# A two-layer decoder trunk: new order of the first loads, shared normalised input for the gate, and regrouped state-output products

## The chip, the cores and the metric

One NeuronCore of a Trainium2 chip runs the whole kernel in one launch. The metric is device time in microseconds (us), lower is better. TensorE, VectorE, ScalarE and GpSimd appear in the profile as PE (matmuls), PEld (weight loads of PE), DVE, ACT and POOL; SP is the engine that issues most DMAs, and its own queue is SPq.

## What is computed

The input x is 256 x 1024 in float32. Layer one is a diagonal complex state-space mixer, layer two an attention mixer over one block of 256 keys. Cut to the first layer, which is what the change touches:

```
hn = rms_norm(x, g)
u, z = split(hn @ w_in)                # 256 x 1024 each
a = exp(dt * (a_re + i a_im))          # 64 groups x 64 states, dt = exp(log_dt)
s = scan(a, f * (u B))                 # state over 256 steps
y = gelu(Re(s C) + d * u)              # back to 1024 channels
y = y * sigmoid(y @ w_glu + b)         # "GLU"
h = x + (y * silu(z)) @ w_out
```

## The kernel before

The program is first recorded, then ordered, then emitted. Every call on an engine handle becomes an `Op` in `Program.add` with a cost in ns from a formula (lines 155 to 176) and its dependences. `Program.order` computes for each Op a priority `way` (six rounds of forward and backward list scheduling in `lay`); `lay` takes on each engine the ready Op with the largest `way`. The emitted order on each engine is fixed from then on, so a change of a cost formula can move instructions anywhere in the kernel, and each engine (and the DMA queue of SP) works strictly in its written order. `fixed()` chains Ops of an engine in the order written; `group()` makes several calls one Op, so that they stay together and wait together.

The first layer runs so. The weights of u (eight 512 KB pieces, `plan` 0 to 7) and of z (8 to 15) go into the buffers `zh` and `zl`, those of later products into `wr`. `x_turn8` transposes x into `xT` (tile `ah`), scaled by the norm gain; `u_step` multiplies it with the u weights in two halves (tiles `uz`). `u_turn` scales each half by the row norms, sends it through four small SBUF-to-SBUF DMAs (`st<-st`) and transposes it into `U`. Meanwhile a chain of small DVE instructions on 128 x 64 tiles turns log_dt, a_re, a_im (transposed by PE into `pt`) into powers of a, and `b_turn` and `c_turn` transpose B and C. For each quarter b of the groups, `x_table` and `y_table` (three 128 x 1024 DVE instructions each, through tile `tb`) make the input and output tables, `x_turn` and `k_table` use them on PE, `ssm_in` multiplies with U, `rotate` does the scan on DVE (ten instructions on the tiles `t1`, `t2`, `t3`, shown as `t`) and sends the state through four DMAs (`st<-t`). `w_table` builds the 64-step convolution table `W` (tile `BW`) by 32 small DMAs (`BW<-um`). `ssm_out` adds two products per output, U with W and the state with Y, in PSUM, transposes and applies gelu. `z_pair` makes z: PE product from `xT`, DVE multiplies it with the row norms (`zz<-uz,rrow`), ACT applies Silu. Then GLU, the output product and layer two follow.

The PSUM tiles `acc`, `uz` and `wide` have two buffers each and take turns in program order. An fp32 matmul stands in the trace as two records.

Of the kernel before, what the change touches and what calls it, by code (L numbers as in the profile page):

```python
# [28 lines left out]
S = 256  # L29
# [11 lines left out]
C_ID, C_PM, C_MK, C_M, C_K, C_CS, C_SG, C_I16, C_RE, C_RU = 0, 128, 192, 320, 384, 388, 516, 518, 534, 536  # L41
# [31 lines left out]
class Op:  # L73
    __slots__ = ("eng", "calls", "cost", "deps", "nbytes", "i", "table", "columns", "parts")


class Program:
# [67 lines left out]
    def add(self, handle, eng, method, a, k):  # L145
# [9 lines left out]
        if dma:  # L155
            cost = self.ISSUE[eng]
        elif eng == "PE":
            if method == "transpose":
                cost = 107 * aps[0].shape[0] / 128
            else:  # L160
                m, c = n(aps[0]), n(aps[1])
                if aps[0].dtype == FR:
                    cost = (2 + max(c, 256) / 2.4) if m == 128 else (28 + max(c, 256) / 2.4) / 2
                else:
                    cost = (4 * max(c, m) / 2.4 + (55 if m < 128 else 2)) * m / 128
                    if m == 32:
                        cost = 47
        elif eng == "DVE":
            two = method in ("tensor_tensor", "scalar_tensor_tensor", "tensor_tensor_scan", "tensor_reduce") or psum
            cost = (70 if not psum else 125) + n(aps[0] if method == "tensor_reduce" else out) * (6.4 if method == "reciprocal" else 1.04 if two else 0.53)  # L170
        elif eng == "ACT":
            cost = 95 + 0.83 * n(aps[0]) + (60 if len(aps) > 1 else 0) + (100 if "accum_out" in k else 0)
        else:
            spread = any(not x.ap[-1][0] for x in aps)
            each = {"memset": 0.85, "tensor_scalar": 5.2}.get(method, 1.8 if spread else 2.2)
            cost = 150 + 205 * n(out) if k.get("op") == OP.pow else 60 + n(out) * each
        if self.open is None:
            op = Op()
            op.eng, op.calls, op.cost, op.deps, op.i = eng, [], 0, {}, len(self.ops)
            op.nbytes, op.table, op.columns, op.parts = 0, None, 0, []  # L180
# [48 lines left out]
    grouping, chain = False, None  # L229
# [26 lines left out]
    def lay(self, after, way, forth):  # L256
# [11 lines left out]
        for _ in ops:  # L268
            t, e = min((max(free[e], min(ready[i] for i in w)), e) for e, w in wait.items() if w)
            able = [i for i in wait[e] if ready[i] <= t]  # L270
            i = max(able, key=lambda i: (way[i] - (4000 if ops[i].table not in (None, table) else 0), -i))
# [21 lines left out]
            if o.nbytes:  # L293
                t += 1120
                if e == "POOL":
                    t = swdge = max(t + 730, swdge + 1480)
                end = max(dma, t) + o.nbytes / 360
                dma = end if e != "POOL" else dma + o.nbytes / 360
# [8 lines left out]
    def order(self):  # L307
# [8 lines left out]
        for o in reversed(ops):  # L316
            own = o.cost + (600 + o.nbytes / 360 if o.nbytes else 0)
            way[o.i] = max([way[j] + (o.cost if lg is None else own + lg) for j, lg in succ[o.i]], default=own)
# [32 lines left out]

TICK, BUSY = 10240 / 3, 3600
# [23 lines left out]
def body(ctx: ExitStack, tc: tile.TileContext, x, norm_g, w_in1, a_re, a_im, log_dt, b_re, b_im,  # L376
# [156 lines left out]
    G.dma_start(vn, ap(norm_g, 0, [[128, 16], [1, 128]]))  # L533
    with prog.fixed():
        w_load(0, 0)
        A.dma_start(cst[:, :C_PM], consts[:, :C_PM])
        x_load(SP, 0, 0, 256)
        x_load(A, 1, 0, 256)
        w_load(0, 1)
        x_load(SP, 0, 256, 512)  # L540
        x_load(SP, 1, 256, 512)
        w_load(1, 0)
        w_load(1, 1)
        x_load(SP, 0, 512, 1024)
        x_load(SP, 1, 512, 1024)
        SP.dma_start(cst[:, C_PM:], consts[:, C_PM:])
# [8 lines left out]
    G.dma_start(ldn, ap(log_dt, 0, [[1, 64], [1, 1]]))  # L555
    for r, w in enumerate((a_re, a_im)):
        G.dma_start(an[:, r], ap(w, 0, [[64, 64], [0, 2], [1, 64]]))
    G.dma_start(vb, ap(b_glu, 0, [[128, 8], [1, 128]]))
# [41 lines left out]
    for k in range(2, 8):  # L600
        x_turn8(k)
    PE.transpose(pt[:, 128:192], bc(ldn, [64, 128]), perm)
    for r in range(2):
        PE.transpose(pt[:, 64 * r:64 * r + 64], an[:, r].rearrange("p d q -> p (d q)"), perm)
    pv0 = acc()
# [87 lines left out]
    def b_turn():  # L693
        for d, r in ((bst, 0), (bsw, 1)):
# [6 lines left out]
    def c_turn():  # L701
        for d, r in ((cst_, 0), (csw, 1)):
# [48 lines left out]
    def u_turn(hf):  # L751
# [139 lines left out]
    def ssm_out(b):  # L891
        p = wide()
        for j2 in range(2):
            rows = slice(64 * j2, 64 * j2 + 64)
            for jl in range(4):
                jp = 4 * b + jl
                with prog.group():
                  for part in range(2):
                    for f in range(2):
                        o = p[64 * f:64 * f + 64, j2 * 512 + jl * 64:j2 * 512 + jl * 64 + 64]  # L900
                        if part == 0:
                            lt, rt = U[rows, jp, 64 * f:64 * f + 64], W[rows, 2 * jp + f]
                        else:
                            lt = PSTS[b][:, jl, j2, 64 * f:64 * f + 64]
                            rt = Y[:, jp * 4 + f * 2 + j2, 1:5].rearrange("p k c -> p (k c)")
                        PE.matmul(o, lt, rt, start=(part == 0), stop=(part == 1))
# [24 lines left out]
    def z_pair(m):  # L931
        p = uz()
        for n in (2 * m, 2 * m + 1):
            load_to(8 + n + 4)
            for k in range(8):
                PE.matmul(p[:, S * (n % 2):S * (n % 2) + S], raw[8 + n][:, 128 * k:128 * k + 128], xT[:, k],
                          start=(k == 0), stop=(k == 7))
        zv = zz[:, 2 * m:2 * m + 2].rearrange("p a b -> p (a b)")
# [10 lines left out]
    act(rrow, pr[:, :S])  # L949
# [314 lines left out]
```

## Time and profile before

| | us |
|---|---|
| three runs | 317.62, 326.90, 327.87 (median 326.90) |
| the profiled execution | 315.07 |
| its span, first to last instruction | 313.0 |
| PE busy, of the span | 293.9 |
| DVE busy | 221.5 |
| ACT busy | 161.1 |
| mean granted TensorE clock | 0.956 |

Times in the views are us from the start of the span. Busy time is the time in which the engine had an instruction under way; "granted clock" is the share of 2.4 GHz that TensorE got in a stretch, 1.00 being the level of 2.4 GHz and 0.50 that of 1.2 GHz. A bracket behind a timeline row gives the idle time before it and what ended that. Line numbers are all 349, the line of `emit`, so rows are told apart by tiles.

### The profile page before, as it was taken

The numbers are of one execution on the slowest core, as the hardware profiler recorded it, in microseconds if no ns is written. First come the engines' busy times: TensorE is split into PE (matmuls) and PEld (weight loads), VectorE is DVE, ScalarE is ACT, GpSimd is POOL, SyncE is SP. The second block draws the span as 40 slices with busy tenths as digits, with TensorE's granted clock in tenths as the row PEclk, the third lists the DMA queues.
The fourth block names the chain that finished last, engine by engine and source line by source line (L and its number), as shares of the span: only waits on it lengthen the run. The fifth ranks groups of instructions, "written<-read, shape, count | busy, mean of one in ns | idle before, by whom it ended". The sixth has DMA issues, their size and how long they took to land.

```text
span 313.0 us, 5398 instructions
## 1 busy us (share of the span) xinstructions
PE 293.9 (94%) x2041; PEld 238.5 (76%) x2041; DVE 221.5 (71%) x408; ACT 161.1 (51%) x315; POOL 20.7 (7%) x33
## 2 busy tenths in 40 slices
PE   7999995999279998999999999999999999999995
PEld 6456464887167675799988888888888889999884
DVE  0006799499999990199765495897785999879713
ACT  2512984663531223197663564657765566677400
POOL 7100100000200000000000000330001300000000
PEclk9999999899757599999999999999999999999999
DMA  7999997022312332674566447375432646252303
GB/s 216 290 293 247 258 261 181 2 69 68 86 27 69 74 81 56 171 241 166 199 202 203 134 139 265 92 251 182 148 134 74 198 134 187 88 199 77 126 0 134
DMA packets 54665, 47.14 MB, mean 151 GB/s; under 512 B 10488, under 2 KB 45200, under 8 KB 54640
## 3 DMA queue, kind: packets, MB, share of 16 engines
q1 hardware_dynamic: 53776, 46.00, 50.9%
q10 hardware_dynamic: 576, 0.72, 0.8%
q8 instruction: 16, 0.26, 0.4%
q0 software_dynamic: 288, 0.08, 0.1%
q14 instruction: 9, 0.07, 0.1%
HBM read 41.94 MB, written 1.05 MB: 137 GB/s over the span
## 4 chain that ended last, share of the span: by engine, by line
PE 73%; DMA 11%; DVE 10%; SPq 2%; ACT 1%; issue 1%; POOL 1%; DVEq 0%; ACTq 0%; POOLq 0%
PE uz L349 35%; PE acc L349 23%; PE wide L349 15%; DVE t L349 7%; DMA zl<-in_ssm_w_in_dram 4%; DMA zh<-in_ssm_w_in_dram 2%; SPq L349 2%; DMA st<-st 1%; DMA st<-t 1%; DMA cst<-consts_dram 1%; DVE tb L349 1%; DVE X L349 1%; ACT yT L349 1%; POOL BW L349 1%; DVE Y L349 1%
## 5 line engine op out<-in xcount | busy, mean ns | idle before, releaser
L349 DVE TENSOR_TENSOR zl<-wr,zh 128x1024 fp32r<-128x1024 f32 x28 | 34.1, 1221 | 10.2 <-ACT zh L349 10.1
L349 ACT ACTIVATE X<-wr 128x1024 fp32r<-128x1024 f32 x28 | 29.6, 1057 | 22.1 <-PE uz L349 9.9
L349 ACT ACTIVATE zh<-wr 128x1024 fp32r<-128x1024 f32 x28 | 29.5, 1058 | 22.2 <-DMA wr<-in_ssm_w_glu_dram 11.6
L349 DVE TENSOR_TENSOR xp<-wr,X 128x1024 fp32r<-128x1024 f32 x28 | 34.1, 1219 | 6.5 <-PE uz L349 4.4
L349 PE MATMUL uz<-ah,zh 128*128 128x256 f32 x96 | 27.7, 389 | 0.0
L349 PE MATMUL uz<-zh,ah 128*128 128x512 f32 x56 | 25.6, 532 | 0.0
L349 PE MATMUL uz<-ah,zl 128*128 128x256 f32 x96 | 25.6, 355 | 0.0
L349 PE MATMUL uz<-zl,ah 128*128 128x512 f32 x56 | 24.7, 511 | 0.0
L349 PEld LDWEIGHTS uz<-ah,zh 128*128 128x128 f32 x96 | 19.4, 211 | 2.7 <-DVE zz L349 0.8
L349 PEld LDWEIGHTS uz<-ah,zl 128*128 128x128 f32 x96 | 17.3, 190 | 1.6
L349 PE MATMUL wide<-BW,U 64*64 64x64 f32 x128 | 12.4, 267 | 3.9 <-DMA BW<-um 3.0
L349 PEld LDWEIGHTS uz<-zh,ah 128*128 128x128 f32 x56 | 10.5, 197 | 6.4 <-issue 5.3
L349 PEld LDWEIGHTS uz<-zl,ah 128*128 128x128 f32 x56 | 10.2, 189 | 6.3 <-issue 5.3
L349 PEld LDWEIGHTS wide<-BW,U 64*64 64x64 f32 x128 | 7.4, 150 | 9.6 <-issue 6.8
L349 DVE TENSOR_TENSOR zz<-uz,rrow 128x512 f32<-128x512 f32 x4 | 4.2, 1102 | 14.6 <-PE uz L349 14.6
L349 ACT ACTIVATE ah<-wide,vec 128x256 f32<-128x256 f32 (+1 forms) x16 | 7.0, 468 | 13.1 <-PE wide L349 13.1
L349 POOL TENSOR_TENSOR sm<-sm,mhalf 128x4 f32<-128x4 f32 x8 | 9.6, 1200 | 51.6 <-DVE sm L349 51.4
L349 PE MATMUL wide<-Y,st 128*64 128x64 f32 x128 | 11.9, 269 | 0.8 <-DMA st<-t 0.8
L349 PEld LDWEIGHTS wide<-U,xp 64*64 64x64 f32 x256 | 9.5, 156 | 1.6 <-issue 0.8
L349 PE MATMUL wide<-U,xp 64*64 64x64 f32 x256 | 10.3, 243 | 0.0
L349 DVE TENSOR_TENSOR t<-t,t 128x512 f32<-128x512 f32 (+1 forms) x16 | 10.2, 675 | 0.0
L349 PE MATMUL acc<-X,ah 128*128 128x512 f32 x24 | 10.1, 421 | 0.0
(270 smaller groups left out, 802.1 us busy)
## 6 DMA issues: line engine op xcount, KB each, us to landing
wr<-in_attn_w_in_dram SPq DMA_DIRECT2D x32, 512.0 KB, 4.0
wr<-in_ssm_w_glu_dram SPq DMA_DIRECT2D x8, 512.0 KB, 6.0
wr<-in_ssm_w_out_dram SPq DMA_DIRECT2D x8, 512.0 KB, 4.0
wr<-in_attn_w_out_dram SPq DMA_DIRECT2D x8, 512.0 KB, 3.4
zh<-in_ssm_w_in_dram SPq DMA_DIRECT2D x8, 256.0 KB, 6.8
zl<-in_ssm_w_in_dram SPq DMA_DIRECT2D x8, 256.0 KB, 6.5
zh<-in_ssm_w_in_dram SPq DMA_DIRECT2D x4, 512.0 KB, 6.0
zl<-in_ssm_w_in_dram SPq DMA_DIRECT2D x4, 512.0 KB, 5.7
```

Of the source, the lines that this page charges most:

```text
L349: getattr(handle, method)(*map(self.real, a), **{q: self.real(v) for q, v in k.items()})
```

## The change

It reorders the columns of the constants, so that the permutation and the small ones stand in the first load; puts the small POOL loads in a fixed order; loads B and C once each (256 KB apiece) and lets ACT copy the real part into the third place; moves them ahead of the weight loads; lifts the priority of the three transposes that start the coefficient chain (`push`); makes every SP DMA written after `u_turn`'s four DMAs follow them in the queue (`behind`); makes z from `xn`, the normalised `xT`, so that Silu reads PSUM itself; and splits `ssm_out` into two groups of 16 products, the first with W over four quadrants of the array, the second with the state. The cost formulas of the planner for fp32 and fp32r matmuls, the scan, POOL DMAs and the DMA rate are changed too.

```diff
-C_ID, C_PM, C_MK, C_M, C_K, C_CS, C_SG, C_I16, C_RE, C_RU = 0, 128, 192, 320, 384, 388, 516, 518, 534, 536
+C_ID, C_PM, C_K, C_SG, C_RE, C_M, C_RU, C_I16, C_CS, C_MK = 0, 128, 192, 196, 198, 200, 264, 520, 536, 664
...
-                    cost = (2 + max(c, 256) / 2.4) if m == 128 else (28 + max(c, 256) / 2.4) / 2
+                    cost = 4 + 0.4455 * max(c, 256)
...
-                    cost = (4 * max(c, m) / 2.4 + (55 if m < 128 else 2)) * m / 128
+                    cost = (4 * c / 2.4 + 2) * m / 128 * aps[0].shape[0] / 128
...
+            if dma and eng == "SP" and self.behind is not None:
+                op.deps[self.behind] = -1
...
-            i = max(able, key=lambda i: (way[i] - (4000 if ops[i].table not in (None, table) else 0), -i))
+            i = max(able, key=lambda i: (way[i] + ops[i].push - (4000 if ops[i].table not in (None, table) else 0), -i))
...
+RATE = 290
...
-    G.dma_start(vn, ap(norm_g, 0, [[128, 16], [1, 128]]))
+    with prog.fixed():
+        G.dma_start(vn, ap(norm_g, 0, [[128, 16], [1, 128]]))
+        G.dma_start(ldn, ap(log_dt, 0, [[1, 64], [1, 1]]))
+        for r, w in enumerate((a_re, a_im)):
+            G.dma_start(an[:, r], ap(w, 0, [[64, 64], [0, 2], [1, 64]]))
...
-        A.dma_start(cst[:, :C_PM], consts[:, :C_PM])
+        A.dma_start(cst[:, :C_RU], consts[:, :C_RU])
...
-        for r, w in enumerate((b_re, b_im, b_re)):
-            if r < 2:
-                load_to(3 + r)
+        for r, w in enumerate((b_re, b_im)):
             SP.dma_start(bn[:, r].rearrange("p q c -> p (q c)"), ap(w, 0, [[1024, 64], [1, 1024]]))
-        for r, w in enumerate((c_re, c_im, c_re)):
+        load_to(4)
+        for r, w in enumerate((c_re, c_im)):
             SP.dma_start(cn[:, :, r], ap(w, 0, [[64, 128], [8192, 8], [1, 64]]))
...
+    prog.push = 20000
     PE.transpose(pt[:, 128:192], bc(ldn, [64, 128]), perm)
...
     def b_turn():
+        act(bn[:, 2], bn[:, 0])
...
     def c_turn():
+        act(cn[:, :, 2], cn[:, :, 0])
...
+        prog.behind = len(prog.ops) - 1
...
+        with prog.group():
+            for jl in range(4):
+                jp = 4 * b + jl
+                for f in range(2):
+                    for j2 in range(2):
+                        rows = slice(64 * j2, 64 * j2 + 64)
+                        product(jl, j2, f, U[rows, jp, 64 * f:64 * f + 64], W[rows, 2 * jp + f], jl == 0, False)
+        with prog.group():
+            for jl in range(4):
+                jp = 4 * b + jl
+                for j2 in range(2):
                     for f in range(2):
...
+                        product(jl, j2, f, PSTS[b][:, jl, j2, 64 * f:64 * f + 64],
+                                Y[:, jp * 4 + f * 2 + j2, 1:5].rearrange("p k c -> p (k c)"), False, jl == 3)
...
-                PE.matmul(p[:, S * (n % 2):S * (n % 2) + S], raw[8 + n][:, 128 * k:128 * k + 128], xT[:, k],
+                PE.matmul(p[:, S * (n % 2):S * (n % 2) + S], raw[8 + n][:, 128 * k:128 * k + 128], xn[:, k],
...
-        tt(V, zz[:, 2 * m:2 * m + 2].rearrange("p a (m s) -> p a s m", s=4), p.rearrange("p (a s m) -> p a s m", a=2, s=4),
-           bc(rrow.rearrange("p (m s) -> p s m", s=4)[:, None], [128, 2, 4, 64]), MUL)
-        act(zv, zv, AF.Silu)
+        act(zz[:, 2 * m:2 * m + 2].rearrange("p a (m s) -> p a s m", s=4), p.rearrange("p (a s m) -> p a s m", a=2, s=4), AF.Silu)
...
+    for k in range(0, 8, 4):
+        tt(V, xn[:, k:k + 4], xT[:, k:k + 4], bc(rrow[:, None, :], [128, 4, S]), MUL)
```

## Rows read from the trace of the kernel before

**Rows 1.** Busy time of the engines in stretches of the span; behind the stretch its length, then PE, PEld, DVE, ACT and POOL with their counts (an engine without work is left out), the granted clock, the DMA share and GB/s.

```profile
26.00:44.40 18.40, 18.40 (x69) 9.94 (x69) 15.56 (x54) 13.74 (x32) 1.13 (x2) 1.00 1.02 246
44.40:62.00 17.60, 14.35 (x146) 12.71 (x148) 13.35 (x13) 11.24 (x26) 0.00 (x0) 0.90 0.51 126
62.00:78.00 16.00, 15.75 (x244) 13.01 (x236) 16.00 (x18) 7.69 (x18) 0.13 (x1) 1.00 0.24 64
78.00:88.00 10.00, 2.06 (x38) 1.53 (x38) 10.00 (x12) 4.88 (x9) 1.81 (x1) 0.68 0.33 75
88.00:103.00 15.00, 14.10 (x184) 11.02 (x186) 15.00 (x17) 3.02 (x6) 0.25 (x2) 0.61 0.23 48
103.00:113.00 10.00, 9.96 (x64) 7.13 (x56) 10.00 (x13) 2.65 (x4) 0.00 (x0) 0.71 0.41 107
113.00:134.60 21.60, 20.77 (x199) 14.55 (x200) 6.96 (x10) 6.75 (x13) 0.13 (x1) 1.00 0.38 89
134.60:158.00 23.40, 23.40 (x198) 23.27 (x196) 19.76 (x36) 18.53 (x37) 0.00 (x0) 1.00 0.63 213
```

**Rows 2.** The timeline up to 62 us: start, length, engine, instruction.

```profile
3.64 0.62 POOL L349 DMA_DIRECT2D Y<-in_ssm_a_im_dram  x1
10.20 0.48 SPq L349 DMA_DIRECT2D Y<-in_ssm_b_im_dram  x1
25.86 0.39 PE L349 MATMUL acc<-cst,Y 64*128 64x64 f32 x3
40.73 0.62 DVE L349 TENSOR_TENSOR s<-t,X 128x192 f32<-128x192 f32 x2
44.22 1.91 PE L349 MATMUL wide<-cst,Y 128*128 128x128 f32 x16
46.01 3.51 SPq L349 DMA_DIRECT2D st<-st  x4
53.68 1.06 ACT L349 ACTIVATE um<-st 128x1024 f32<-128x1024 f32 x1 [3.86 <-DMA st<-st]
61.95 1.22 DVE L349 TENSOR_TENSOR t<-wide,EC 128x1024 f32<-128x1024 f32 x1 [4.07 <-PE wide L349]
```

**Rows 3.** The page's DMA issues: queue, count, size of one, median us from issue to landing.

```profile
st<-t SPq DMA_DIRECT2D x16, 128.0 KB, 2.4
Y<-in_ssm_b_im_dram SPq DMA_DIRECT2D x1, 256.0 KB, 8.1
Y<-in_ssm_a_im_dram POOLq DMA_DIRECT2D x1, 32.0 KB, 4.4
```

**Rows 4.** DVE's instructions on tile `t` (the ten of each `rotate`) in the stretch from the first rotate to the last: length, busy time with count, granted clock, DMA share, GB/s.

```profile
61.90:116.10 54.20, 37.80 (x40) 0.78 0.28 68
```

**Rows 5.** The other large groups of DVE in the same stretch: shape and count, busy us, mean ns, idle time before.

```profile
L349 DVE TENSOR_TENSOR tb<-s,yT 128x1024 f32<-128x1024 f32 x2 | 2.4, 1216 | 0.0
L349 DVE TENSOR_TENSOR Y<-Y,tb 128x1024 f32<-128x1024 f32 x2 | 2.4, 1216 | 0.0
L349 DVE TENSOR_TENSOR X<-X,tb 128x1024 f32<-128x1024 f32 x2 | 2.4, 1216 | 0.0
L349 DVE TENSOR_TENSOR Y<-s,yT 128x1024 f32<-128x1024 f32 x2 | 2.4, 1206 | 0.0
L349 DVE TENSOR_TENSOR tb<-s,BW 128x1024 f32<-128x1024 f32 x1 | 1.2, 1214 | 0.0
L349 DVE TENSOR_TENSOR X<-s,BW 128x1024 f32<-128x1024 f32 x1 | 1.2, 1211 | 0.0
L349 DVE TENSOR_TENSOR zz<-uz,rrow 128x512 f32<-128x512 f32 x2 | 2.1, 1080 | 0.0
```

**Rows 6.** PE in the timeline: `ssm_in` of one quarter, a `k_table`, a long row of z products, and the alternation of `ssm_out` and z products.

```profile
59.82 2.08 PE L349 MATMUL wide<-U,xp 64*64 64x64 f32 x64
61.83 0.65 PE L349 MATMUL acc<-Y,X 128*32 128x64 f32 x32
72.73 5.01 PE L349 MATMUL uz<-ah,zl 128*128 128x256 f32 x22
...
128.67 0.34 PE L349 MATMUL wide<-Y,st 128*64 128x64 f32 x4
128.93 0.33 PE L349 MATMUL wide<-BW,U 64*64 64x64 f32 x4
...
129.46 1.13 PE L349 MATMUL uz<-ah,zl 128*128 128x256 f32 x4
130.52 0.33 PE L349 MATMUL wide<-BW,U 64*64 64x64 f32 x4
```

**Rows 7.** The timeline around the end of the state-space part: z's normalisation, the last rotate, SP's queue, the last product with the state.

```profile
102.33 2.07 DVE L349 TENSOR_TENSOR zz<-uz,rrow 128x512 f32<-128x512 f32 x2
103.46 3.06 PE L349 MATMUL uz<-ah,zh 128*128 128x256 f32 x6
114.74 1.27 DVE L349 TENSOR_TENSOR t<-t,t 128x504 f32<-128x504 f32 x2
118.17 6.40 SPq L349 DMA_DIRECT2D BW<-um  x8
124.61 1.30 SPq L349 DMA_DIRECT2D st<-t  x2
134.01 0.34 PE L349 MATMUL wide<-Y,st 128*64 128x64 f32 x4
```

More of the change, by code (lines that the diff above doesn't have):

```diff
@@ L73 @@
 class Op:
-    __slots__ = ("eng", "calls", "cost", "deps", "nbytes", "i", "table", "columns", "parts")
+    __slots__ = ("eng", "calls", "cost", "deps", "nbytes", "i", "table", "columns", "parts", "push")
 class Program:
@@ L162, in add @@
                 if aps[0].dtype == FR:
-                    cost = (2 + max(c, 256) / 2.4) if m == 128 else (28 + max(c, 256) / 2.4) / 2
+                    cost = 4 + 0.4455 * max(c, 256)
                 else:
-                    cost = (4 * max(c, m) / 2.4 + (55 if m < 128 else 2)) * m / 128
+                    cost = (4 * c / 2.4 + 2) * m / 128 * aps[0].shape[0] / 128
                     if m == 32:
-                        cost = 47
+                        cost = 42
         elif eng == "DVE":
             two = method in ("tensor_tensor", "scalar_tensor_tensor", "tensor_tensor_scan", "tensor_reduce") or psum
-            cost = (70 if not psum else 125) + n(aps[0] if method == "tensor_reduce" else out) * (6.4 if method == "reciprocal" else 1.04 if two else 0.53)
+            cost = (70 if not psum else 125) + n(aps[0] if method == "tensor_reduce" else out) * (6.4 if method == "reciprocal" else 2.1 if method == "tensor_tensor_scan" else 1.04 if two else 0.53)
         elif eng == "ACT":
@@ L179, in add @@
             op.eng, op.calls, op.cost, op.deps, op.i = eng, [], 0, {}, len(self.ops)
-            op.nbytes, op.table, op.columns, op.parts = 0, None, 0, []
+            op.nbytes, op.table, op.columns, op.parts, op.push = 0, None, 0, [], self.push
             self.ops.append(op)
@@ L228, in add @@
             self.seen[name] = keep
-    grouping, chain = False, None
+    grouping, chain, behind, push = False, None, None, 0
     @contextmanager
@@ L295, in lay @@
                 if e == "POOL":
-                    t = swdge = max(t + 730, swdge + 1480)
-                end = max(dma, t) + o.nbytes / 360
-                dma = end if e != "POOL" else dma + o.nbytes / 360
+                    t = swdge = max(t + 1500, swdge + 600)
+                end = (t if e == "POOL" else max(dma, t)) + o.nbytes / RATE
+                dma = end if e != "POOL" else dma + o.nbytes / RATE
             stop[i] = free[e]
@@ L316, in order @@
         for o in reversed(ops):
-            own = o.cost + (600 + o.nbytes / 360 if o.nbytes else 0)
+            own = o.cost + (600 + o.nbytes / RATE if o.nbytes else 0)
             way[o.i] = max([way[j] + (o.cost if lg is None else own + lg) for j, lg in succ[o.i]], default=own)
@@ L531, in w_load @@
         SP.dma_start(raw[i].rearrange("p (k f n) -> p k f n", k=2, f=2)[:, k], src[:, k])
[L533 removed]
+    with prog.fixed():
[3 more added lines that the diff above has]
+            G.dma_start(an[:, r], ap(w, 0, [[64, 64], [0, 2], [1, 64]]))
+        G.dma_start(vb, ap(b_glu, 0, [[128, 8], [1, 128]]))
     with prog.fixed():
         w_load(0, 0)
[L536 removed]
+        A.dma_start(cst[:, :C_RU], consts[:, :C_RU])
         x_load(SP, 0, 0, 256)
@@ L542, in body @@
         w_load(1, 0)
-        w_load(1, 1)
         x_load(SP, 0, 512, 1024)
         x_load(SP, 1, 512, 1024)
-        SP.dma_start(cst[:, C_PM:], consts[:, C_PM:])
+        w_load(1, 1)
+        SP.dma_start(cst[:, C_RU:C_I16], consts[:, C_RU:C_I16])
         bn = nat[:64, 0:3072].rearrange("p (r q c) -> p r q c", r=3, c=16)
         cn = nat[:, 3072:4608].rearrange("p (b r q) -> p b r q", b=8, r=3)
-        for r, w in enumerate((b_re, b_im, b_re)):
-            if r < 2:
-                load_to(3 + r)
+        for r, w in enumerate((b_re, b_im)):
             SP.dma_start(bn[:, r].rearrange("p q c -> p (q c)"), ap(w, 0, [[1024, 64], [1, 1024]]))
-        for r, w in enumerate((c_re, c_im, c_re)):
+        load_to(4)
+        for r, w in enumerate((c_re, c_im)):
             SP.dma_start(cn[:, :, r], ap(w, 0, [[64, 128], [8192, 8], [1, 64]]))
[L555 to L558, printed above, removed]
+        load_to(5)
+        SP.dma_start(cst[:, C_I16:], consts[:, C_I16:])
     dk = small([128, 16])
@@ L604, in body @@
         PE.transpose(pt[:, 64 * r:64 * r + 64], an[:, r].rearrange("p d q -> p (d q)"), perm)
+    prog.push = 0
     pv0 = acc()
@@ L892, in ssm_out, with product @@
         p = wide()
-        for j2 in range(2):
-            rows = slice(64 * j2, 64 * j2 + 64)
+        def product(jl, j2, f, lt, rt, start, stop):
+            o = p[64 * f:64 * f + 64, j2 * 512 + jl * 64:j2 * 512 + jl * 64 + 64]
+            PE.matmul(o, lt, rt, start=start, stop=stop, skip_group_check=True)
+        with prog.group():
             for jl in range(4):
                 jp = 4 * b + jl
-                with prog.group():
-                  for part in range(2):
-                    for f in range(2):
[L900 to L906, printed above, removed]
+                for f in range(2):
[6 more added lines that the diff above has]
+                for j2 in range(2):
+                    for f in range(2):
+                        product(jl, j2, f, PSTS[b][:, jl, j2, 64 * f:64 * f + 64],
+                                Y[:, jp * 4 + f * 2 + j2, 1:5].rearrange("p k c -> p (k c)"), False, jl == 3)
         ys = tile_([128, 4, 8, 16], F, name="ys", bufs=2)
@@ L948, in body @@
     rrow = tile_([128, S], F, name="rrow")
-    act(rrow, pr[:, :S])
+    act(rrow.rearrange("p (s m) -> p s m", s=4), pr[:, :S].rearrange("p (m s) -> p s m", s=4))
+    xn = tile_([128, 8, S], F, name="al")
+    for k in range(0, 8, 4):
+        tt(V, xn[:, k:k + 4], xT[:, k:k + 4], bc(rrow[:, None, :], [128, 4, S]), MUL)
     for k in range(8):
```

1 line of the change is left out of this document (removed).

## The prediction

> **What bounds the kernel now.** I read the busy time by stretches first [rows 1]. From 26.0 to 44.4 us PE is busy all the time: this is the product for u, and no load holds it up. From 62 to 113 DVE is busy without a gap, and PE is not: 2.06 us of work in the ten from 78 to 88, and a granted clock of 0.68, 0.61 and 0.71 up to 113, so most of that time at 1.2 GHz. From 113 to 134.6 it is the other way round: DVE works 6.96 of 21.6 us, PE 20.77. From 134.6 on PE is full again. So one engine after the other sets the pace between 44 and 135, and there each has work that could stand beside the other's.
>
> Then the timeline before 62 us [rows 2]. The coefficient chain on DVE begins when PE has transposed log_dt, a_re and a_im at 25.86 and ends at 40.73 + 0.62 = 41.35. Its inputs were there much earlier: the last POOL load was issued at 3.64 and landed 4.4 us later [rows 3], at 8. Only then can the tables begin. U is late for another reason: the four DMAs of the second `u_turn` are issued from 46.01 to 49.52, ACT gets them at 53.68, and the first rotate starts at 61.95, after DVE sat idle for 4.07.
>
> Third, what DVE does from there to the last rotate's end at 114.74 + 1.27 = 116.0 [rows 4, 5, 7]: 40 instructions of the rotates, 37.8 us; ten table instructions (2 + 2 + 2 + 2 + 1 + 1) at 1.21, 12.1 us; two normalisations of z, 2.1 us. Fourth, PE at the end [rows 6, 7]: z's third pair resumes only at 103.46, when DVE has emptied the two `uz` buffers at 102.33 and after. So half of z stands behind a DVE instruction of low urgency.
>
> **The coefficient chain and the tables.** Started right behind its last input, the chain may begin at 8 + 0.5 and, at its old length of 15.5, end at 24; I take 25. B's load landed at 10.20 + 8.1 = 18.3 before [rows 2, 3]; two loads and 0.5 MB are gone and it stands ahead of four weight pieces, so it is earlier, not later. The two ACT copies for the third place cost about 1.1 and half of that, by the 1.06 of a 1024-wide copy [rows 2]; ACT is free for a quarter of this stretch [rows 1]. Each of the eight tables takes three instructions. Buffers let three X tables and all four Y tables run before U is there; the fourth X table needs the first one's buffer. Seven tables are 21 x 1.21 = 25.5 us, with `xn` (two 1024-wide multiplications, 2.4) and small work of 2 some 30: from 25 to 55, inside the time to the first rotate. So three instructions instead of ten stay behind: 7 x 1.21 = 8.5 us off the DVE stretch. Bounds: 0, if the planner leaves C's transposes (1.91 us, at 44.22 before [rows 2]) where they are, and 8.5. I take 8.5, since PE can place 1.9 us before 44.
>
> **The shared normalised input.** It takes 2.1 us off the same stretch and adds 2.4 before it, where DVE is idle. More important, Silu empties PSUM on ACT, which works 3.02 of 15 us there [rows 1]; z's second half, 64 records at 5.01/22 = 0.228 us [rows 6], 14.6 us, can go into PE's gaps. Its cover is ACT's idle time; without it z waits as today. The new wait, z on `xn`, lies at about 30, long before z starts.
>
> **Late weight loads.** Behind `u_turn`'s DMAs stand now z's and GLU's weights, later qkg and gcol. Issue took 3.51 and landing about 4.2 (49.52 to 53.68) with those in front; the rotates' DMAs, with an emptier queue, land in 2.4 [rows 2, 3]. That is 0.9 + 1.8 = 2.7 us earlier at best; C's transposes before the end of u take 1.9 of it at worst. I take 2. The weights that wait are used from 46 (z, eight pieces) and 113 on (GLU); the DMA engines are half free from 44 to 62 and mostly free after [rows 1], which covers them. What would be late next: z pieces 12 to 15, a few us, while PE has U's transposes and `ssm_in`.
>
> **The two groups of products.** Before, every pair of matmuls with W, then with the state, takes 0.26 us (128.67 to 128.93 [rows 6]): 16 such pairs, 4.2 us a quarter. In `ssm_in` two quadrants overlap: 32 matmuls in 2.08, 0.065 each. Four quadrants at that rate give 16 x 0.0325 = 0.52, two column halves 16 x 0.065 = 1.04: 1.6 instead of 4.2, 10.4 us over four quarters. Bounds: 0, if nothing overlaps, and 10.4. I take the upper: in `k_table` 32 records with four column groups took 0.65 [rows 6], 0.02 each. The row suggests why the pairs are slow: four z records between them take 1.06 (129.46 to 130.52), not 4 x 0.228 = 0.91, so each change of shape costs about 0.15. The Trainium skill, TensorEngine Tiling, Key Properties, says that a change of tiling mode drains the engine; the trace agrees, with these 0.15 us. The same page's Instruction Overhead allows about 60 cycles to every matmul, an estimate of 25 ns, which would make the first group 0.8 and take 1.1 us from the sum; `k_table`'s 0.02 speaks against it.
>
> Before, a pair waited for the state too; now the first group waits only for W and U, and holds its `wide` buffer until the state is there. The buffers already change hands in this order, so nobody new waits for it.
>
> **Sum.** The last rotate ends at 116.0 - 8.5 - 2.1 - 2 = 103.4. Then four DMAs at 0.65 (1.30 for two [rows 7]) 2.6, landing 2.4, second group 1.04: 109.4. The W DMAs that stood ahead of the last state (6.40 us from 118.17 [rows 7]) go earlier with the tables. Before, this point was 134.01 + 0.34 = 134.35. So DVE allows 25 us. PE: the six stretches from 44.4 to 134.6 hold 76.99 us of work [rows 1]; the three slow ones are 26.12, or 17.07 at full clock, so 67.9 in all, and 57.5 without the 10.4. After 62, 57.5 - 14.35 = 43.1 remain; at the 0.78 granted before [rows 4] they end at 62 + 55.3 = 117.3, a gain of 17; at full clock at 105. So 17 to 25; I take 19, near PE's end, because the order that the planner gives can't be seen. From 134.6 on PE is full and its work unchanged; the new costs may shift that by 3 us either way. 315.07 - 19 = **296** for an execution like the profiled one. The three runs shown lie 0.8, 3.8 and 4.1% above it; I put the forecast 1.7% above, **301 us**.
>
> **The rivals.** (1) PE takes over: nothing overlaps in the new groups and the clock stays at 0.78. Then 67.9 - 14.35 = 53.5 us after 62 become 68.6 and end at 130.6: a gain of 4, 311 (316 on the runs' scale), no change that can be told; 2% is about what a measurement can tell here. For it: PE had 45 us of work in DVE's stretch already. Against it: `k_table`. Chance 0.13. (2) In between: only part is gained, because the tables slip behind u's product or z is placed late; 7 to 12 us, 303 to 308 (308 to 313 on that scale), still over 2%. Chance 0.17. (3) The slower end: less PE work in DVE's stretch keeps the engine at 1.2 GHz to its end. The trace has such a stretch: after the idle 78 to 88 the clock was 0.61 although PE then worked 14.1 of 15 us [rows 1]. At 0.5 the 43.1 us take 86 and end at 148: 13.6 late, 329. It decides below 43.1/72.6 = 0.59. The Trainium skill, TensorE: Matmul & The Clock Gate, Why this matters for your kernels, says that idle gaps bring the half clock back; by that rule this rival, and the trace agrees as far as 0.61. Against it: z and the early groups fill those gaps. Chance 0.08. (4) That the change doesn't move the chain (its transposes could still stand late in PE's order) is in (2): then the rotates end at 112, and PE decides.
>
> The forecast, a gain of 13 to 25, has 0.62. The range: 315 - 27 = 288 with all of DVE's gain and 2 from the later order; 313 is a gain of 14.5 at 4.1% above, or the middle of (2). Faster by over 2%: 0.62 + 0.17 = 0.79; within: 0.13; slower: 0.08.
>
> **What would show it.** The first DVE instruction of the chain near 9 instead of 26, and tables before 30; ACT's `um` copy at 51 to 52; at most four table instructions after the first rotate; `zz<-uz` on ACT alone, and z's last record before 105; `ssm_out`'s first group in 0.5 to 0.6 us and the second in about 1.0; a granted clock above 0.8 from 78 to 113; the first GLU matmul at 110 to 118. The forecast is wrong if the tables stay behind U, if PE's clock falls below 0.6 there, or if what is gained before GLU is lost in layer two.

## The result and the profile after

The changed kernel took 297.5 us (median of 4 runs, 296.01 to 299.7) beside 322.26 us (median of 4, 316.97 to 327.87) for the kernel before; the ratio is 0.938 [0.925, 0.951]. Executions of one kernel fall into a fast and a slow state, and every ratio here is of the fast ones alone (of the kernel before 316.97 and 317.62), so it is not the quotient of the medians. The forecast was 301 us in a range of 288 to 313. The profiled execution took 296.01 us, with a span of 293.9 and a mean granted clock of 0.977: 19.1 us less than the 315.07 of before, where the sum of the prediction said 19.

Busy time in stretches of the changed kernel, columns as in [rows 1]; the edges follow its own stages.

```profile
26.00:44.40 18.40, 18.40 (x64) 9.53 (x64) 18.20 (x17) 12.66 (x26) 0.72 (x1) 1.00 0.52 143
44.40:60.00 15.60, 15.60 (x206) 13.66 (x206) 12.46 (x12) 7.17 (x13) 1.81 (x1) 1.00 0.92 230
60.00:78.00 18.00, 18.00 (x223) 15.42 (x222) 17.66 (x20) 9.43 (x22) 0.35 (x3) 1.00 0.50 116
78.00:88.00 10.00, 10.00 (x150) 8.32 (x152) 6.60 (x9) 3.79 (x6) 0.00 (x0) 1.00 0.44 107
88.00:103.00 15.00, 7.86 (x133) 6.11 (x133) 11.74 (x16) 8.34 (x16) 0.13 (x1) 0.82 0.26 55
103.00:113.00 10.00, 8.12 (x124) 7.05 (x126) 8.91 (x22) 1.72 (x3) 0.13 (x1) 0.58 0.64 162
113.00:118.00 5.00, 5.00 (x64) 4.93 (x61) 1.75 (x5) 3.84 (x11) 0.00 (x0) 1.00 1.15 327
```

From 26 us on PE now works without a gap at full clock to 88 us; the stretch that held 2.06 us of work in ten before [rows 1] holds ten. Its gap has moved to 88 to 113, and the low clock with it. From 113 on PE is full, which it was from 134.6 on before [rows 1].

The timeline up to the first rotate, to be read beside [rows 2].

```profile
8.88 0.22 DVE L351 TENSOR_SCALAR t<-acc 128x64 f32<-128x64 f32 x1 [2.95 <-PE acc L351]
25.02 2.78 DVE L351 TENSOR_TENSOR X<-s,BW 128x1024 f32<-128x1024 f32 x2
45.18 2.56 SPq L351 DMA_DIRECT2D st<-st  x4
49.62 1.06 ACT L351 ACTIVATE um<-st 128x1024 f32<-128x1024 f32 x1 [3.48 <-DMA st<-st]
57.47 1.22 DVE L351 TENSOR_TENSOR t<-wide,EC 128x1024 f32<-128x1024 f32 x1
```

The coefficient chain begins at 8.88, the tables at 25.02, inside u's product. The first rotate comes 4.48 us earlier: U's DMAs are issued 0.83 earlier and in 0.95 less, land 2.28 sooner (from the end of the issue to ACT's start 49.62 - 47.74 = 1.88 instead of 4.16), and 0.42 is gained between the copy and the rotate.

DVE from the first rotate to the last: the instructions of the rotates as in [rows 4], then all engines, with the columns of [rows 1].

```profile
57.40:106.90 49.50, 37.53 (x40) 0.91 0.42 97
...
57.40:106.90 49.50, 40.47 (x554) 33.70 (x553) 42.25 (x50) 23.51 (x46) 2.42 (x6) 0.91 0.42 97
```

All engines in the same stretch of the kernel before, from its first rotate to its last:

```profile
61.90:116.10 54.20, 45.06 (x538) 34.86 (x537) 54.15 (x61) 19.30 (x38) 2.32 (x5) 0.78 0.28 68
```

The groups of the changed kernel in its stretch that wait or are left over, and the longest waits; the columns of the first rows are those of [rows 5].

```profile
L351 DVE TENSOR_TENSOR t<-wide,EC 128x1024 f32<-128x1024 f32 x4 | 4.9, 1217 | 2.4 <-ACT EC L351 2.2
L351 DVE TENSOR_TENSOR t<-wide,ES 128x1024 f32<-128x1024 f32 x4 | 4.9, 1216 | 3.4 <-DMA st<-t 3.4
L351 DVE TENSOR_TENSOR X<-X,tb 128x1024 f32<-128x1024 f32 x1 | 1.2, 1222 | 0.0
```

One table instruction of the ten in [rows 5] stays. The rotates are as long as before, and DVE, which was busy for 54.15 of 54.20 us, now stands idle for 49.50 - 42.25 = 7.25: 3.4 for the state's DMAs, 2.2 for ACT's `EC`, the rest in small pieces.

The timeline from 64 us to the end of the state-space part: SP's queue, the products of `ssm_out`, z's last, ACT's copy of it and of `EC`, the rotates.

```profile
64.50 12.46 SPq L351 DMA_DIRECT2D BW<-um  x16
77.08 17.76 SPq L351 DMA_DIRECT2D st<-t  x12
81.69 1.23 DVE L351 TENSOR_TENSOR t<-wide,ES 128x1024 f32<-128x1024 f32 x1 [3.40 <-DMA st<-t]
81.79 0.69 PE L351 MATMUL wide<-BW,U 64*64 64x64 f32 x32
82.42 0.65 PE L351 MATMUL acc<-Y,X 128*32 128x64 f32 x32
83.00 1.15 PE L351 MATMUL wide<-Y,st 128*64 128x64 f32 x32
84.08 0.68 PE L351 MATMUL wide<-U,xp 64*64 64x64 f32 x16
90.69 0.70 PE L351 MATMUL uz<-al,zl 128*128 128x256 f32 x2
91.42 1.13 ACT L351 ACTIVATE zz<-uz 128x512 f32<-128x512 f32 x1 [1.11 <-PE uz L351]
92.34 0.64 ACT L351 ACTIVATE EC<-ES 128x512 f32<-128x512 f32 x1
94.64 1.22 DVE L351 TENSOR_TENSOR t<-wide,EC 128x1024 f32<-128x1024 f32 x1 [2.23 <-ACT EC L351]
105.55 1.27 DVE L351 TENSOR_TENSOR t<-t,t 128x504 f32<-128x504 f32 x2
106.37 3.03 SPq L351 DMA_DIRECT2D st<-t  x4
108.57 1.13 PE L351 MATMUL wide<-BW,U 64*64 64x64 f32 x32
109.63 1.91 PE L351 MATMUL wide<-Y,st 128*64 128x64 f32 x32
111.47 0.69 PE L351 MATMUL wide<-BW,U 64*64 64x64 f32 x32
112.64 1.15 PE L351 MATMUL wide<-Y,st 128*64 128x64 f32 x32
```

DVE's wait for `EC` comes from ACT's order: the copy stands behind the Silu of z's last pair, for which ACT waits until PE is done with z at 91.4, though DVE had made the copy's input by 89.96. So z's end reaches the last rotate.

The first group takes 82.42 - 81.79 = 0.63 from its start to the next instruction's, the second 84.08 - 83.00 = 1.08; while the clock is low, 1.06 and 1.84 (108.57 to 109.63 to 111.47). z is done at 91.4. The last state product ends at 112.64 + 1.15 = 113.8, before at 134.35 [rows 7]: 20.6 us earlier, of which 19.1 reach the end. Of the 1.5 given back, 1.4 is seen in layer two, where PE waits for an ACT and a DVE split that it did not wait for before; the kernel before with the new formulas alone (p_costs) shows the same two waits:

```profile
PE acc L351 <- ACT ah L351: 0.8, 1, 0.8
PE acc L351 <- DVE al L351: 0.6, 1, 0.6
```

### The profile page after: what moved, and what is told of

It reads as the page before. It is cut to its first block, busy times and chain, and to the rows that moved or that the text cites. A ratio compares the mean times of both kernels' runs of the same rounds, so it can differ in the third digit from the quotient of the medians.

```text
span 293.9 us, 5383 instructions
## 1 busy us (share of the span) xinstructions
PE 278.1 (95%) x2041; PEld 228.0 (78%) x2041; DVE 219.9 (75%) x406; ACT 162.2 (55%) x316; POOL 22.3 (8%) x33
## 4 chain that ended last, share of the span: by engine, by line
PE 80%; DVE 7%; DMA 6%; ACT 3%; issue 3%; POOL 0%; ACTq 0%; POOLq 0%; SPq 0%; DVEq 0%
PE uz L351 40%; PE acc L351 23%; PE wide L351 17%; DMA wr<-in_attn_w_in_dram 4%; DVE t L351 2%; DVE xp L351 2%; DMA Y<-in_norm_g_dram 1%; DVE zl L351 1%; ACT X L351 1%; DVE sm L351 1%; DVE D L351 1%; DVE Y L351 1%; ACT L351 0%; ACT ys L351 0%; DVE al L351 0%
## 5 line engine op out<-in xcount | busy, mean ns | idle before, releaser
L351 PE MATMUL uz<-al,zh 128*128 128x256 f32 x96 | 23.8, 348 | 0.0
L351 PEld LDWEIGHTS uz<-al,zh 128*128 128x128 f32 x96 | 18.0, 190 | 1.6
L351 PE MATMUL uz<-al,zl 128*128 128x256 f32 x64 | 16.5, 387 | 0.0
L351 PE MATMUL uz<-ah,xp 128*128 128x256 f32 x32 | 10.0, 311 | 3.3 <-DVE xp L351 3.3
L351 PEld LDWEIGHTS uz<-al,zl 128*128 128x128 f32 x64 | 11.4, 190 | 1.5
L351 PE MATMUL uz<-al,X 128*128 128x256 f32 x32 | 10.3, 322 | 1.8 <-DVE al L351 1.8
L351 PE MATMUL uz<-ah,X 128*128 128x256 f32 x32 | 10.2, 317 | 1.9 <-ACT ah L351 1.9
L351 ACT ACTIVATE U<-D 128x256 fp32r<-128x256 f32 x16 | 6.5, 416 | 8.7 <-DVE D L351 8.7
L351 PE MATMUL acc<-X,al 128*128 128x512 f32 x24 | 9.6, 398 | 0.6 <-DVE al L351 0.6
L351 PE MATMUL acc<-zh,ah 128*128 128x512 f32 x24 | 9.9, 413 | 0.0
```

The costliest lines, as they stand in the source:

```text
L351: getattr(handle, method)(*map(self.real, a), **{q: self.real(v) for q, v in k.items()})
```

## The experiments

My theory was the sum of the prediction: loads and tables, z, late weights and groups each take their term off one path. The rivals were that a part has slack and is worth nothing, that the new cost formulas do it by themselves, or that a part works by another way than its term says. The table gathers all runs: median, ratio to the kernel before run beside it (for f_mixed no ratio was taken; its two runs are 311.8 and 316.58), and of the profiled execution the span and three points. The changed kernel's own four executions lie between 296.01 and 299.7, so a difference of up to 4 us between two single executions can be spread.

| run | median us | ratio to before | span | first rotate | last rotate ends | last state product ends |
|---|---|---|---|---|---|---|
| before | 322.26 | | 313.0 | 61.95 | 116.0 | 134.35 |
| after | 297.5 | 0.938 [0.925, 0.951] | 293.9 | 57.47 | 106.8 | 113.8 |
| u_loads | 309.29 | 0.976 [0.969, 0.983] | 307.0 | 58.18 | 118.7 | 126.1 |
| u_groups | 307.42 | 0.975 [0.943, 1.007] | 303.3 | 59.88 | 110.8 | 122.4 |
| u_behind | 304.69 | 0.964 [0.958, 0.971] | 301.6 | 65.26 | 109.8 | 120.0 |
| u_z | 300.14 | 0.952 [0.941, 0.962] | 298.0 | 60.41 | 106.9 | 119.1 |
| u_push | 296.64 | 0.941 [0.922, 0.959] | 293.6 | 55.33 | 103.8 | 112.6 |
| f_behind | 306.55 | 0.972 [0.957, 0.987] | 303.8 | 66.90 | 116.2 | 123.3 |
| f_mixed | 314.19 | | 309.7 | 57.40 | 111.6 | 127.4 |
| p_costs | 317.65 | 1.006 [1.001, 1.010] | 311.9 | 66.08 | 109.0 | 129.1 |
| p_oldcosts | 306.19 | 0.964 [0.949, 0.980] | 304.4 | 59.27 | 114.2 | 126.9 |
| i_push_st | 297.12 | 0.936 [0.918, 0.954] | 296.5 | 61.00 | 105.1 | 115.1 |
| i_act_st | 302.78 | 0.953 [0.938, 0.969] | 301.1 | 62.78 | 107.5 | 123.4 |
| i_merge_w | 300.09 | 0.949 [0.941, 0.958] | 297.0 | 62.00 | 107.3 | 115.4 |

Runs named u_ undo one part and let the planner order everything anew; f_ keep the changed kernel's order word for word, but for the part in question; p_ separate formulas and moves; i_ try to improve.

**The loads (u_loads).** The old constants, POOL loads, triple loads of B and C and no lifted priority; all else stays changed. The cut shows three places of the edit.

```diff
-        A.dma_start(cst[:, :C_RU], consts[:, :C_RU])
+        A.dma_start(cst[:, :C_PM], consts[:, :C_PM])
...
-        for r, w in enumerate((b_re, b_im)):
+        for r, w in enumerate((b_re, b_im, b_re)):
...
-    prog.push = 20000
...
```

> The changed kernel with the first loads as before: constants in the old column order with the permutation in the second, late piece, B and C loaded three times each behind two weight pieces, POOL's loads unordered, no lift of the three transposes; products in groups, z from the normalised input, late weight loads and new cost formulas stay. Theory A (the tables' early start is a part of its own): the chain starts near 19 as in the run with the cost formulas alone, the first table stands near 35, some 8 us of table work go back behind the first rotate or in front of it, the last rotate ends 4 to 9 us later than 106.8 and the time is 301 to 306 us. Rival B (the chain has slack, as the run without the lift showed, whose chain began at 15.05): the first table comes 10 us late but the tables end before U is there all the same; first rotate within 2 us of 57.47, last rotate within 2 us of 106.8, time 295 to 300 us.

Measured: span 307.0, 13.1 us above the changed kernel's, more than the first theory said. Three rows of the timeline and the longest wait of PE (total, times, longest).

```profile
23.20 0.23 DVE L351 TENSOR_SCALAR t<-acc 128x64 f32<-128x64 f32 x1 [7.32 <-PE acc L351]
98.42 1.22 DVE L351 TENSOR_TENSOR Y<-Y,tb 128x1024 f32<-128x1024 f32 x1
117.38 1.27 DVE L351 TENSOR_TENSOR t<-t,t 128x504 f32<-128x504 f32 x2
...
PE acc L351 <- DVE X L351: 9.6, 1, 9.6
```

The chain begins at 23.20, eleven table instructions stand between the first rotate and the last, the last of them at 98.42, and the last rotate ends 11.9 us later. PE waits 9.6 us for an X table. DVE works 55.56 us between the first rotate and the last, 13.3 more than in the changed kernel. The second half of `xn` is among that, at 76.41, so z is late too (117.4 instead of 91.4). Of the parts undone one at a time this cost most, but its times (307.29 to 310.8) overlap those of u_groups (305.19 to 309.65).

**The lift of the three transposes (u_push).**

```diff
-    prog.push = 20000
+    prog.push = 0
```

> Undoes one part: no raised priority for the three transposes that start the coefficient chain; the planner puts them behind four u steps. Theory A (the chain's start carries through the tables to the rotates): the chain starts about 7 us later, at 16, the first table at about 32, three or four more table instructions fall behind the first rotate, and the time rises by 3 to 6 us, to 299 to 302. Theory B (there is slack before U arrives): the tables are still ready, the time stays within 1.5 us of 296.

Measured: the chain began at 15.05 instead of 8.88, the first table at 29.15, and nothing got later. So the chain has slack of at least 6 us: it need not begin at 8.88. In u_loads it begins at 23.20 and the first table follows right behind it, at 38.74; that this, and not another of the late loads there, makes u_loads slow is likely, but was not tried alone.

**Products in pairs (u_groups, f_mixed).** u_groups takes the old `ssm_out` back; f_mixed keeps the order of the changed kernel, but issues both groups' products pair by pair at the place of the second; the cut is f_mixed's.

```diff
+    def mixed(self, first, second):
...
+                for f in range(2):
+                    h, m, args, k = first[4 * jl + 2 * f + j2]
+                    calls.append((h, m, args, dict(k, start=True, stop=False)))
+                for f in range(2):
+                    h, m, args, k = second[4 * jl + 2 * j2 + f]
+                    calls.append((h, m, args, dict(k, start=False, stop=True)))
...
```

> Undoes one part: the state-output products stand in pairs again (W, state, W, state), all else as changed, ordered anew. Theory A (up to about 107 us DVE and the waits behind it set the pace, PE has room): PE gets some 10 us more work between 80 and 115, but it stood idle there for about 9 us and worked at a lowered clock, so the time rises by only 2 to 6 us, to 298 to 302, and the last rotate ends within 2 us of 106.8. Theory B (PE's work is what was saved): the whole 10 us come back, 306. Both expect about 0.26 us per pair of matmuls at full clock.

> The order of the changed kernel is kept on every engine; only where the second group of an ssm_out stands, both groups are issued pair by pair (W, W, state, state) as before the change. Theory E (the cost of the pairs is PE time behind the last state, where nothing covers it: the last two quarters stand at 108 to 114 in one row): 16 pairs at 0.26 are 4.2 us a quarter instead of 1.6, so 2 x 2.6 at full clock and up to 2 x 4 at half clock, 5 to 8 us, 301 to 304, and the last rotate moves by less than 2 us. Theory F (most of the 9.4 us that undoing the groups cost lay in the new order that the planner made for them): under 3 us.

Measured in f_mixed: pairs at full clock, the first and the last pair of the last two quarters, ACT's wait and DVE's, and the busy time around them.

```profile
82.31 0.33 PE L367 MATMUL wide<-BW,U 64*64 64x64 f32 x4
82.57 0.34 PE L367 MATMUL wide<-Y,st 128*64 128x64 f32 x4
96.17 1.11 ACT L367 ACTIVATE zz<-uz 128x512 f32<-128x512 f32 x1 [4.25 <-PE uz L367]
99.38 1.23 DVE L367 TENSOR_TENSOR t<-wide,EC 128x1024 f32<-128x1024 f32 x1 [7.63 <-ACT EC L367]
113.31 0.48 PE L367 MATMUL wide<-BW,U 64*64 64x64 f32 x4
113.72 0.48 PE L367 MATMUL wide<-Y,st 128*64 128x64 f32 x4
126.96 0.48 PE L367 MATMUL wide<-Y,st 128*64 128x64 f32 x4
...
113.00:123.00 10.00, 10.00 (x91) 7.09 (x92) 3.65 (x14) 0.66 (x2) 0.00 (x0) 0.50 0.80 201
```

A step takes 0.26 us at full clock and 0.41 at half, so a quarter 16 x 0.26 = 4.2 and 16 x 0.41 = 6.6 us, instead of 0.63 + 1.08 = 1.7. The first two quarters push z's last products back on PE, so ACT waits for them until 96.17 instead of 91.42, and `EC` stands behind them in ACT's order: DVE waits 7.63 instead of 2.23, and the last rotate ends 4.8 later. Then two quarters in pairs at half clock follow it: 111.6 to 127.4 is 15.8 us instead of 7.0. Both together are the 13.6 us by which the last state product is later; the span is 15.8 longer. In u_groups, where the planner made room for the longer products, 9.4 us of span are lost, 4.0 of them before the last rotate's end, 4.6 between it and the last state product. So of u_groups' theories B, with 306, came nearer; of f_mixed's both missed, E because the last rotate did move. f_mixed also makes the products with W wait for the state, as in the kernel before, so its 15.8 us price more than the change of shape.

**z from the plain transposed input (u_z).** Behind the cut, DVE's normalisation from PSUM and Silu from SBUF come back as they were.

```diff
-                PE.matmul(p[:, S * (n % 2):S * (n % 2) + S], raw[8 + n][:, 128 * k:128 * k + 128], xn[:, k],
+                PE.matmul(p[:, S * (n % 2):S * (n % 2) + S], raw[8 + n][:, 128 * k:128 * k + 128], xT[:, k],
...
```

> Undoes one part: z from the plain transposed x again, normalised by DVE from PSUM, then Silu from SBUF; ordered anew. Theory A (DVE's stretch sets the pace): DVE gets four instructions of 1.08 us after U instead of two of 1.22 before, and z again waits for DVE to empty PSUM: 3 to 8 us slower, 299 to 304, the last rotate ends 2 to 4 us later. Theory B (DVE has slack now, 6.60 of 10 us busy from 78 to 88): no change, 296 to 297.

Measured: 4.1 us of span; the medians differ by 2.6, and the two runs (300.04 and 300.25) lie just above the changed kernel's slowest, so the size is unsure. The first rotate starts 2.9 later and the last still ends at 106.9, as without the edit, so the 2.1 us on DVE that the prediction counted don't show. What shows is PE: z's second half resumes only at 92.95, after DVE has emptied both `uz` buffers (88.09 to 90.09), from then on PE has no gap, and the last state product stands late in that row.

```profile
107.77 2.76 PE L351 MATMUL uz<-ah,zl 128*128 128x256 f32 x12
117.94 1.15 PE L351 MATMUL wide<-Y,st 128*64 128x64 f32 x32
```

z ends at 110.5 instead of 91.4, the last state product at 119.1 instead of 113.8.

**Late weight loads (u_behind, f_behind).** u_behind drops the rule and plans anew (the cut's first line); f_behind puts the six weight loads that follow the four DMAs in SP's queue ahead of them and changes nothing else (the rest).

```diff
-        prog.behind = len(prog.ops) - 1
...
+        sp = [o for o in ops[first:] if o.eng == "SP" and o.i not in self.turn_dmas][:6]
+        names = {o.i for o in sp}
+        rest = [o for o in ops if o.i not in names]
+        at = [i for i, o in enumerate(rest) if o.i in self.turn_dmas][0]
+        return rest[:at] + sp + rest[at:]
```

> Undoes one part: weight loads may stand ahead of u_turn's DMAs again; ordered anew, the planner puts four GLU loads, a z load and four small loads ahead of the first u_turn and four z loads ahead of the second. Theory A (U's arrival sets the first rotate and is carried to the end): ACT gets the second turned u 2 to 4 us later than at 49.62, the end moves by as much, 298 to 300. Theory B (DVE has other work then): under 1.5 us.

> The order of the changed kernel is kept on every engine; only on SP's queue six weight loads (three of z, three of GLU) are put ahead of the second u_turn's four DMAs. Theory A (the loads in front delay U, and U's arrival sets the first rotate): ACT gets the turned u 3 us or more later than at 49.62 (six loads of 512 KB are 3 MB, over 10 us at 290 GB/s if all lie in front: up to 60), and the end moves by about the same, 3 to 10 us. Theory B (DVE has other work then and catches up): under 1.5 us.

Measured in f_behind, with U's DMAs, the copy behind them and the first rotate:

```profile
48.82 3.59 SPq L359 DMA_DIRECT2D st<-st  x4
57.24 1.06 ACT L359 ACTIVATE um<-st 128x1024 f32<-128x1024 f32 x1 [10.65 <-DMA st<-st]
66.90 1.23 DVE L359 TENSOR_TENSOR t<-wide,EC 128x1024 f32<-128x1024 f32 x1
```

The issue starts 3.64 later and takes 1.03 more, but landing takes 57.24 - 52.41 = 4.83 us instead of 1.88. So the copy comes 7.6 later, the last rotate 9.4, the span is 9.9 longer: U's arrival is on the path in full. f_behind is harder than the kernel before at this place: three GLU loads stand right in front of the four DMAs (issued from 45.34), where that one had issued its GLU loads from 26.08 on. u_behind lost 7.7, more than its theory A said; ACT's copy came 6.5 later there.

**Formulas alone, moves alone (p_costs, p_oldcosts).** p_costs is the kernel before with the new cost formulas and `RATE = 290` only; p_oldcosts is the changed kernel with the old ones, as here.

```diff
-                    cost = 4 + 0.4455 * max(c, 256)
+                    cost = (2 + max(c, 256) / 2.4) if m == 128 else (28 + max(c, 256) / 2.4) / 2
...
-                    cost = (4 * c / 2.4 + 2) * m / 128 * aps[0].shape[0] / 128
+                    cost = (4 * max(c, m) / 2.4 + (55 if m < 128 else 2)) * m / 128
...
```

> The kernel before with the changed cost formulas of the planner and nothing else: the same instructions, another order. Theory A (the gain comes from what is moved and saved): 0 to 5 us faster than before's 315 to 317, and the coefficient chain still starts after 20. Theory C (the gain is the planner's: with truer costs it finds the order by itself): 10 us or more faster, under 306.

> The changed kernel ordered with the old cost formulas. Theory A: keeps most of the gain, 296 to 302. Theory C: loses most of it, over 306.

Measured: the formulas alone gave nothing (ratio 1.006, span 1.1 us shorter); the chain began at 19.12, a little before the 20 expected. The moves without them gave 8.6 of the 19.1 us of span, with 306.19 us outside theory A's 296 to 302: in the order made by the old formulas DVE stands idle ahead of the tables. So 9.4 us come only when both stand together, and neither theory holds alone.

```profile
43.66 1.23 DVE L351 TENSOR_TENSOR tb<-s,BW 128x1024 f32<-128x1024 f32 x1 [11.12 <-ACT BW L351]
```

**Three tries at the state's DMAs (i_push_st, i_act_st, i_merge_w).** In the changed kernel the state stands in SP's queue behind 16 DMAs of W. The first state was complete at 71.90 + 1.26 = 73.2, not at 69.7 as the first expectation has it, and was issued at 77.08. The edits lift its priority in the planner, issue it from ACT, or halve the number of W's DMAs, in this order in the cut.

```diff
+        prog.push = 20000
...
-                SP.dma_start(st[64 * ri:64 * ri + 64, :, j2],
+                A.dma_start(st[64 * ri:64 * ri + 64, :, j2],
...
-        jp = slice(8 * hf, 8 * hf + 8)
+        jp = slice(0, 16)
...
```

> The changed kernel, with raised priority for the four state DMAs of each rotate, so that they are issued between the small DMAs of the W table instead of behind all sixteen. In the changed kernel DVE waited 3.40 us at 81.69 for state DMAs that stood behind W's (issued at 77.08, the first state was ready at 69.7). Theory A (this wait is on the path): it goes, the last rotate ends 2 to 4 us earlier than 106.8, the time falls by 1 to 4 us, to 292 to 295. Theory D (W's table is late instead, and ssm_out with it): no gain or a loss of up to 3 us.

> The changed kernel, with the state DMAs issued by ACT instead of SP. Theory A: as with raised priority, the 3.40 us wait goes, 1 to 4 us faster. Theory D: ACT, in order, stands waiting for DVE's last rotate instruction before each and its evictions of PSUM come late: the same or up to 5 us slower.

> The changed kernel with the W table sent in 16 DMAs over all quarters instead of two sets of 16 (the same bytes). SP gets 10 us less to issue, and the state DMAs of the first two quarters stand ahead of W's. Theory G (SP's queue is what holds the last part: DVE's wait of 3.40 us and W's second half at 94.94 to 105.24): the last state product ends 2 to 5 us earlier than 113.7, 291 to 295. Theory D (the first quarters' products wait for all of W and PE is late instead): the same or up to 3 us slower.

Measured: none was faster. With the state lifted it is issued at 77.75 in the middle of W's DMAs, DVE waits for it no more, and PE waits for W instead; issued from ACT, PE waits longer still. Waits of PE up to the end of the state-space part in the two:

```profile
77.75 2.72 SPq L351 DMA_DIRECT2D st<-t  x4
...
PE wide L351 <- DMA BW<-um: 5.1, 3, 3.2
```

```profile
PE wide L351 <- DMA BW<-um: 7.5, 4, 4.2
```

With 16 instead of 32 DMAs for W the same wait was 6.4 us. These too were planned anew, with first rotates 3.5 to 5.3 us later, so they don't price DVE's wait alone. In i_push_st DVE did gain: from a start 3.5 later its last rotate ends 1.7 earlier. Yet the last state product comes 1.3 later, since PE needs W as well as the state. No version beat the changed kernel by more than its runs spread; u_push equals it.

## Why the prediction was right, step by step

**Size and way.** Forecast and measurement agree for the profiled execution, 19 and 19.1 us; the 301 was put 1.7% above its 296, and the median lies 0.5% above. The likeliest case was the one that came: tables before U, PE full at full clock up to 88 us, the state-space part's end 20.6 us earlier. That 19 and 19.1 meet so closely is luck: 19 was picked between 17 by PE and 25 by DVE, and several terms were off in both directions and cancelled. One term is missing. The sum gave the new formulas at most 3 us, behind 134.6; with the old ones the same moves keep only 8.6 of the 19.1 us (p_oldcosts).

**Tables: 8.5 us forecast.** Nine instructions of ten left the stretch; with the two normalisations of z, DVE works 54.15 - 42.25 = 11.9 us less, where 10.6 was counted. The chain began at 8.88 (forecast 9), the first table at 25.0 (25). u_loads confirms the part and shows more than its term, 13.1 us, with a late z in it.

**z: 2.1 us on DVE, and its products into gaps.** u_z bears out the second half of that step; the first doesn't show there. `zz<-uz` is on ACT alone and z ends at 91.4, before 105 as said. The cover, ACT's idle time, was not complete: the Silu of z's last pair holds up `EC`, and DVE waits 2.2 us.

**U's arrival: 2 us taken, 2.7 at best.** Of the gains this one was most undersized: 4.48. The issue was 0.95 shorter and began 0.83 earlier, and the landing took 1.88 instead of 4.16, so that the copy came at 49.6 and not at 51 to 52. The step compared two measures: the 2.4 of [rows 3] runs from each DMA's own issue to its landing, the 4.2 from the end of the last issue. By the first measure these four DMAs took 5.0 before and 2.4 now, in the median. Undoing it costs more than the gain (9.9 in f_behind), since the loads stand closer in front there and hold up issue and landing.

**Two groups: 0.52 + 1.04 a quarter.** Measured 0.63 and 1.08 at full clock, and 1.06 and 1.84 in one quarter at the lowered one: 3 x 1.71 + 2.90 = 8.0 us for four quarters, where 6.2 was forecast and the pairs of before take 16.8 at full clock. The rows of f_mixed show the price of changing shape: 4.2 instead of 1.7 us for the same 32 matmuls, in 16 steps of two, so (4.2 - 1.7)/16 = 0.16 a change at most, as the pairs also use two quadrants where the group uses four. The prediction had 0.15 from another row. The Trainium skill, TensorEngine Tiling (Array Packing), Key Properties, says that a change of mode drains the engine; the trace agrees, with up to 0.16 us. By the Trainium skill, the same page, Instruction Overhead, about 60 cycles a matmul, the estimate was 0.8 for the first group; the trace, with 0.63, stays below it and decides. What failed in this step is its place: I put the groups into PE's work that is hidden behind DVE and let them matter through PE's end alone. f_mixed shows two other ways: through z's end and ACT's order, on to `EC` and the fourth rotate, and through the last two quarters that stand behind the last rotate at half clock.

**Last rotate at 103.4.** It ended at 106.8. 4.5 us from U and 11.9 of work make 99.6; the 7.2 us of new waits, which the sum did not have, give 106.8. The prediction asked who waits for `wide`, and not what the state would stand behind in SP's queue: all of W's first half, 64.50 to 76.96. Three tries to take that wait away gave no gain, each in a newly planned order.

**Last state product at 109.4.** 113.8 measured, 7.0 instead of 6.0 behind the last rotate, so the miss is mostly the rotate's. PE's end, put between 105 and 117.3 by the clock, came there too. The first GLU matmul was to come at 110 to 118; it stands at 98.05, with others in PE's gaps behind it, and only from 113.72 on is PE full again.

**The clock.** It was to be above 0.8 from 78 to 113, and was for 25 of these 35 us; from 103 to 113 it was 0.58, after PE had worked 7.86 of 15 us. That is under the 0.6 that the prediction named as a sign against itself. So the slower rival's mechanism is there in small: less PE work leaves a gap, and what follows runs near the level of 1.2 GHz. The Trainium skill, TensorE: Matmul & The Clock Gate, Why this matters for your kernels, says that idle gaps bring the half clock back; the trace agrees, with the 0.58. The lower clock cost about 1.2 us on one quarter's groups (2.90 - 1.71) and something on the GLU products before them, not the 13.6 of that rival, because only 8.1 us of work lay there.

**The others.** That PE takes over did not happen, since the groups overlap, nor that the chain stays where it was. Layer two shifted by 1.5 us, within the 3 allowed.

**The parts don't add.** Undone one at a time they cost 13.1, 9.4, 7.7, 4.1 and nothing, 34 us of span against a gain of 19.1. Each undo was planned anew, so each number holds what the planner then did with the rest; f_behind and f_mixed, without that, cost more still, and the formulas, undone in p_oldcosts, another 10.5. The points of the table show where this comes from: f_behind gives up all of DVE's gain (its last rotate ends at 116.2, before at 116.0) and still keeps 9.2 us of span, p_costs brings the last rotate to 109.0, 7.0 earlier than before, and gains 1.1 us of span: 20.1 instead of 18.3 us follow it up to the last state product, in pairs, and 4.1 more are lost behind that, where PE is busy for 177.3 instead of 175.0 us and idle for 5.5 instead of 3.7. The end needs an early last rotate and a short way from there. How much of the loads' and of z's number is the planner's order and how much the part stays open; it was not tried.

## What to carry to other kernels

Cost a stage by its two ends: when its last producer is done, and what stands between that and the last consumer; a term that shortens one of them is worth what the other leaves. For small transfers on the path, count what lies ahead of them in the queue twice, for the issue and for the landing. A wait that shows in the profile is worth removing only when nothing else is due at the same time, and a run that removes it and keeps the rest of the order would tell; the three tries here were planned anew. Where a planner orders the kernel, change its formulas and the program together and apart: here neither gave half of the gain alone.

## What the runs showed of the hardware

Four SBUF-to-SBUF DMAs of 128 KB each had landed 1.88 us after the end of their issue in the changed kernel and 4.83 with six more weight loads ahead of them (f_behind), while their issue grew from 2.56 to 3.59: the landing took the larger part. Sixteen matmuls of 64 x 64 x 64 over four quadrants took 0.63 us, 0.04 each, while such products in turns, two and two, with ones of 128 x 64 cost 0.13 a matmul of either kind, and 0.2 at the lowered clock.
